# A four-layer decoder trunk on one core: norm vectors and the first stream block loaded through ScalarE's queue, weights first on SP's, the first weight block's high part copied by VectorE, ten warming products

## The chip, the core and the metric

The kernel runs on one core of a Trainium2 chip. The metric is the device time of one execution in microseconds (us); the times shown are medians of several executions. The core has five engines that run their own instruction lists in order and wait for each other through semaphores: TensorE (PE in the profile: PE is the matmul, PEld the load of its stationary operand), VectorE (DVE), ScalarE (ACT), GpSimd (POOL) and SyncE (SP). SP computes nothing here; it issues transfers between the chip's main memory and the on-chip memory. ScalarE can issue transfers too, from its own instruction list.

## The reference

A residual stream of 256 positions by 1024 features passes through four layers. Each layer normalises the stream, runs a token mixer, adds the result, normalises again, runs a squared-ReLU MLP of width 4096 and adds again. The mixers are, in turn, differential attention (layers 0 and 3), block-sparse attention (layer 1) and sliding-window attention (layer 2). Everything is float32.

```python
def rms_norm(x, g):
    xf = x.astype(jnp.float32)
    y = xf * lax.rsqrt(jnp.mean(xf * xf, axis=-1, keepdims=True) + NORM_EPS)
    return (y * g.astype(jnp.float32)).astype(x.dtype)

def sqrelu_mlp(h, w_up, w_down):
    a = jnp.maximum(h @ w_up, 0)
    return (a * a) @ w_down

def reference(x, positions, ...):
    cos, sin = rope_tables(positions)
    h = x
    for i in range(DEPTH):
        a = rms_norm(h, attn_norm_g[i])
        ...
        h = h + y
        h = h + sqrelu_mlp(rms_norm(h, mlp_norm_g[i]), mlp_w_up[i], mlp_w_down[i])
    return rms_norm(h, final_norm_g)
```

## The kernel before

The stream is kept transposed: features on the 128 partitions, positions along the free axis, as eight blocks of 128 features by 256 positions, two to a tile (`hT`, 128 by 512). The weights lie in main memory as pieces of 128 by 2048 in the order in which they are used, and are streamed through four buffers named `raw`.

Every product is made in three parts to keep float32's accuracy. `stage` (L153) splits a piece of weights into a high part `whi`, which ScalarE copies from `raw` in a reduced float32 format (L162), and a low part `wlo`, the difference, which VectorE computes (L163). `norm_part` (L309) does the same for a block of the stream: ScalarE multiplies it by its gain into the high part of `hg` (L315), VectorE computes the low part (L316). TensorE then adds high by high, low by high and high by low in one accumulator. The scale of the norm is applied after the product: `norm_sum` (L318) squares the stream on ScalarE (`sq`, L320) and adds on VectorE (`acc`, L325 and L329); `mean_square` makes `p_sum` and `nx` (L338), and GpSimd the factor `nr` (L291).

What matters here is the start of the program. SP issues, in this order: the norm vectors with the positions (`gn`, L197); then eight times a quarter of a weight piece (128 by 512, L148) followed by one block of the stream (128 by 256, L191), which makes pieces 0 and 1 and all eight blocks; then pieces 2 and 3 in halves (128 by 1024), and whole pieces from there on. Transfers take one of eight semaphores in turn, so from the ninth on an issue waits for the landing of the one eight before it. In the meantime VectorE begins the rotary tables (L239 to L254), which need `gn`, and GpSimd fills masks, constants and the zero halves of the key tiles (`kpadh`, `kpadl`, L456). TensorE multiplies a tile of ones by itself into `p_warm`, WARM = 12 times, and then starts the first projection `p_in` (L107, `proj` L362). The first projection runs feature block by feature block, six products for each (both halves of the positions with each of the three parts); call these groups 0 to 7. Group k needs quarter k of pieces 0 and 1 and block k of the stream. The second projection needs pieces 2 and 3, two feature blocks for each half-piece; I call the halves 2a, 2b, 3a and 3b.

The order on each engine is set by a scheduler when the program is built. `TURNS` (L36) adds, layer by layer, pairs of TensorE instructions of which the first must stand behind the second; instructions are counted by the accumulator that they write.

Of the kernel before, what the change touches and what calls it, by code (L numbers as in the profile page):

```python
# [27 lines left out]
NEG = -1.0e38  # L28
LOOK = 2
FAR = 5  # L30
WARM = 12
RAW = 4


# [14 lines left out]
        (("p_qk", 24), ("p_d", 5)),  # L49
        (("p_s", 40), ("p_d", 36)),  # L50
        (("p_t", 21), ("p_d", 66)),
    ),
    1: (
        (("p_sum", 0), ("p_in", 31)),
# [36 lines left out]

def f(ap):
    return ap.bitcast(F32)


class Numbered:
# [25 lines left out]
def trunk(ctx: ExitStack, tc: tile.TileContext, xT, gains, lams, swa_row, fng, weights, out):  # L122
# [18 lines left out]
    def fetch(parts=1, along=None):  # L141

        i = len(fetched)
        raw = sb.tile([P, 2048], F32, tag="raw", name=f"raw{i}", bufs=RAW)
        w = 2048 // parts
        for h in range(parts):
            s = slice(h * w, (h + 1) * w)
            nc.sync.dma_start(raw[:, s], weights[i, :, s])  # L148
            if along:
                along()  # L150
        fetched.append(raw)

    def stage(w=1024, first=None):  # L153
        i = len(staged)
        raw = fetched[i]
        hi = sb.tile([P, 2048], F32R, tag="whi", name=f"whi{i}", bufs=LOOK + 1)
        lo = sb.tile([P, 2048], F32R, tag="wlo", name=f"wlo{i}", bufs=LOOK + 1)
        for h in range(2048 // w):
            if first:
                first()  # L160
            s = slice(h * w, (h + 1) * w)
            A.activation(hi[:, s], raw[:, s], AF.Copy)  # L162
            V.tensor_tensor(lo[:, s], raw[:, s], f(hi[:, s]), op=OP.subtract)  # L163
        staged.append((hi, lo))

    used = [0]

    def take():
        i = used[0]
# [16 lines left out]
    posi = gn[:, 2 * DEPTH * 8 + 2:].bitcast(I32)  # L186
    loaded = []

    def load_x():
        d = len(loaded)  # L190
        nc.sync.dma_start(hT[d // 2][:, S * (d % 2):S * (d % 2) + S], xv[:, d, :])  # L191
        loaded.append(d)

    first_act = cst.tile([P, 1], F32, name="first_act")
    V.memset(first_act, 0.0)
    A.activation(first_act, first_act, AF.Copy)
    nc.sync.dma_start(gn, gains)  # L197
    fetch(4, load_x)
    fetch(4, load_x)
    fetch(2)  # L200
    fetch(2)

# [33 lines left out]
    def rotary_tables():  # L236
# [8 lines left out]
        for turn, bits in ((2.0 ** 16 * math.pi, 10), (2.0 * math.pi, 9), (2.0 * math.pi, 20)):  # L245
            q = cst.tile([P, NT, 8], F32, name="turns")
            V.tensor_scalar(q, an, 1.0 / turn, None, op0=OP.mult)
            V.tensor_scalar(q, q, 12582912.0, None, op0=OP.add)
            V.tensor_scalar(q, q, -12582912.0, None, op0=OP.add)
            for x in (an, an, lo):  # L250
                m, e = math.frexp(turn)
                c = math.ldexp(math.floor(m * 2 ** bits), e - bits)
                turn -= c
                V.scalar_tensor_tensor(x, q, -c, x, op0=OP.mult, op1=OP.add)  # L254
            if bits == 10:
                yield
            V.scalar_tensor_tensor(lo, q, -turn, lo, op0=OP.mult, op1=OP.add)
            if bits != 20:
                V.tensor_tensor(q, an, lo, op=OP.add)
                V.tensor_tensor(an, an, q, op=OP.subtract)  # L260
                V.tensor_tensor(lo, an, lo, op=OP.add)
                V.tensor_copy(an, q)
# [46 lines left out]
    def norm_part(n, d):  # L309

        j, b = d // 2, d % 2
        if b == 0:
            n.both.append(sb.tile([P, 2, 2, S], F32R, tag=f"hg{j}", name=f"hg{j}", bufs=1))
        both, h, g = n.both[j][:, b], hT[j][:, S * b:S * b + S], n.gain[:, d:d + 1]
        A.activation(both[:, 0], h, AF.Copy, scale=g)  # L315
        V.scalar_tensor_tensor(both[:, 1], h, g, f(both[:, 0]), op0=OP.mult, op1=OP.subtract)  # L316

    def norm_sum(n, j):  # L318
        sq = sb.tile([P, 512], F32, tag="relu", name="sq")
# [679 lines left out]
```

## Time and profile before

| what | value |
|---|---|
| median of 3 executions | 1141.2 us (1141.0 to 1141.56) |
| the profiled execution | 1141.6 us, span 1139.8 us |
| TensorE busy | 1130.4 us (99%) |
| VectorE busy | 826.2 us (72%) |
| ScalarE busy | 660.3 us (58%) |
| transfers | 198.66 MB, mean 174 GB/s |

The profile is one execution; times in it are counted from the start of its span. Each row of a timeline gives a start, a duration, the engine, the line of the kernel and the tiles as output<-inputs, and in brackets how long the engine had been idle and what released it. The profile's matmuls are pipelined and their ends are modelled, so a row of 0.39 us does not mean that the next product starts 0.39 us later; where it matters, the distance from start to start is used.

### The profile page before, as it was taken

Reading aid. Unit: us, or ns where it says so; the run is one execution under the profiler, and the core shown is the slowest. Engines: PE = TensorE matmul, PEld = TensorE weight load, DVE = VectorE, ACT = ScalarE, POOL = GpSimd, SP = SyncE. Lnnn points to the kernel's source line nnn. Section 1 sums busy time; section 2 is a strip of 40 time slices with the busy share of each in tenths; the row PEclk is TensorE's granted clock in tenths of the full one; section 3 lists DMA queues with packets and bytes.
Section 4 is the critical chain, followed back from the end, with each engine's and each line's share of the span. In section 5 each row is a group of like instructions: output and inputs, shape, how many; then the busy total and the mean of one; then the engine's idle time right before and its main releaser. Section 6 shows DMA issues by size and latency. Waiting matters only on the chain.

```text
span 1139.8 us, 17024 instructions
## 1 busy us (share of the span) xinstructions
PE 1130.4 (99%) x6560; PEld 982.9 (86%) x6560; DVE 826.2 (72%) x1584; ACT 660.3 (58%) x1207; POOL 13.2 (1%) x43
## 2 busy tenths in 40 slices
PE   9999999999999999999999999999999999999997
PEld 7889888888888888888899998888888889888886
DVE  7888977656676698766569887775667788777453
ACT  7866656544476665554446865554446776665342
POOL 2000000000000000000000000000000000000000
PEclk9999999999999999999999999999999999999999
DMA  8543455555544355555563346555554444554551
GB/s 321 206 148 116 171 198 193 196 198 185 185 148 148 112 185 188 188 200 191 194 209 111 112 149 222 185 185 187 189 197 139 144 142 162 197 195 168 185 185 37
DMA packets 30608, 198.66 MB, mean 174 GB/s; under 512 B 3520, under 2 KB 5184, under 8 KB 7360
## 3 DMA queue, kind: packets, MB, share of 16 engines
q1 hardware_dynamic: 30240, 197.06, 50.2%
q8 instruction: 51, 0.84, 0.3%
q10 hardware_dynamic: 288, 0.52, 0.1%
q14 instruction: 29, 0.24, 0.1%
HBM read 196.52 MB, written 1.05 MB: 173 GB/s over the span
## 4 chain that ended last, share of the span: by engine, by line
PE 94%; DVE 2%; DMA 1%; ACT 1%; issue 1%; SPq 0%; POOL 0%; POOLq 0%; DVEq 0%
PE p_up L107 31%; PE p_down L107 23%; PE p_in L107 18%; PE p_last L107 7%; PE p_d L107 6%; PE p_s L107 3%; PE p_av L107 2%; PE p_t L110 1%; DMA raw<-in_weights 1%; DVE wlo L163 1%; PE p_e L107 1%; PE p_qk L110 1%; ACT whi L162 0%; DVE kpadl L569 0%; ACT qk L680 0%
## 5 line engine op out<-in xcount | busy, mean ns | idle before, releaser
L163 DVE TENSOR_TENSOR wlo<-raw,whi 128x1024 fp32r<-128x1024 f32 (+1 forms) x374 | 446.5, 1210 | 201.8 <-ACT whi L162 200.9
L162 ACT ACTIVATE whi<-raw 128x1024 fp32r<-128x1024 f32 (+1 forms) x374 | 383.8, 1046 | 209.8 <-issue 110.5
L107 PE MATMUL p_up<-hg,whi 128*128 128x512 f32 x1024 | 356.1, 394 | 0.0
L107 PE MATMUL p_up<-hg,wlo 128*128 128x256 f32 x1024 | 283.1, 277 | 0.0
L107 PE MATMUL p_down<-uu,whi 128*128 128x512 f32 x768 | 266.4, 394 | 0.0
L107 PEld LDWEIGHTS p_up<-hg,whi 128*128 128x128 f32 x1024 | 191.8, 188 | 43.9
L107 PE MATMUL p_in<-whi,hg 128*128 128x512 f32 (+1 forms) x736 | 213.0, 371 | 0.4 <-ACT hg L315 0.4
L107 PE MATMUL p_down<-uu,wlo 128*128 128x256 f32 x768 | 212.7, 277 | 0.0
L107 PEld LDWEIGHTS p_up<-hg,wlo 128*128 128x128 f32 x1024 | 192.3, 188 | 0.5
L107 PEld LDWEIGHTS p_down<-uu,whi 128*128 128x128 f32 x768 | 144.0, 188 | 33.5
L107 PEld LDWEIGHTS p_in<-whi,hg 128*128 128x128 f32 x736 | 131.6, 189 | 24.0 <-ACT hg L315 1.1
L107 PEld LDWEIGHTS p_down<-uu,wlo 128*128 128x128 f32 x768 | 144.1, 188 | 0.0
L107 PE MATMUL p_in<-wlo,hg 128*128 128x512 f32 (+1 forms) x368 | 130.5, 368 | 0.6 <-DVE wlo L163 0.5
L107 PE MATMUL p_d<-oo,whi 128*128 128x256 f32 (+1 forms) x416 | 85.2, 296 | 0.0
L785 ACT ACTIVATE uu<-u 128x512 fp32r<-128x512 f32 x64 | 40.5, 632 | 73.5 <-DVE u L783 73.5
L107 PEld LDWEIGHTS p_in<-wlo,hg 128*128 128x128 f32 x368 | 68.8, 189 | 12.4 <-DVE wlo L163 1.5
L107 PE MATMUL p_last<-whi,uu 128*128 128x512 f32 (+1 forms) x264 | 79.4, 383 | 0.0
L705 ACT ACTIVATE cross<-p_up 128x256 f32<-128x256 f32 x128 | 47.9, 374 | 37.3 <-PE p_up L107 35.3
L107 PEld LDWEIGHTS p_d<-oo,whi 128*128 128x128 f32 x416 | 66.5, 191 | 2.5 <-issue 0.3
L315 ACT ACTIVATE hg<-hT,gn 128x256 fp32r<-128x256 f32 x64 | 31.4, 503 | 61.2 <-DVE hT L718 61.2
L426 ACT ACTIVATE e<-ns,nm 128x128 f32<-128x128 f32 (+1 forms) x128 | 56.7, 446 | 13.8 <-DVE nm L423 13.8
L107 PE MATMUL p_d<-oo,wlo 128*128 128x256 f32 x224 | 63.6, 287 | 0.0
(168 smaller groups left out, 1072.1 us busy)
## 6 DMA issues: line engine op xcount, KB each, us to landing
raw<-in_weights SPq DMA_DIRECT2D x181, 1024.0 KB, 4.9
raw<-in_weights SPq DMA_DIRECT2D x8, 256.0 KB, 4.6
raw<-in_weights SPq DMA_DIRECT2D x4, 512.0 KB, 7.8
hT<-in_xT SPq DMA_DIRECT2D x8, 128.0 KB, 4.5
bias<-in_swa_row SPq DMA_DIRECT2D x1, 512.0 KB, 3.7
grow<-in_fng SPq DMA_DIRECT2D x1, 512.0 KB, 3.5
out<-res SPq DMA_DIRECT2D x4, 128.0 KB, 2.1
out<-res ACTq DMA_DIRECT2D x2, 256.0 KB, 2.2
```

What stands on the lines that cost most here:

```text
L107: return self.keep(out.tensor.name.rstrip("_0123456789"), self.engine.matmul(out, *args, **kw))
L110: return self.keep(out.tensor.name.rstrip("_0123456789"), self.engine.transpose(out, *args, **kw))
L162: A.activation(hi[:, s], raw[:, s], AF.Copy)
L163: V.tensor_tensor(lo[:, s], raw[:, s], f(hi[:, s]), op=OP.subtract)
L315: A.activation(both[:, 0], h, AF.Copy, scale=g)
L426: A.activation(e[:, s], ns[:, s], AF.Exp, bias=nm[:, t:t + 1], scale=-1.0, accum_out=l[:, t:t + 1])
L705: A.activation(cross, p[:, S:], AF.Copy)
L785: A.activation(both[:, :, 0], r3(2)(u), AF.Copy)
```

## The change

Five things are changed, all of them at the program's start:

- `gn` and block 0 of the stream are issued by ScalarE, ahead of its first activation; SP's list begins with the first two quarters of weights, and a block of the stream follows each later quarter. SP has two transfers less to issue, and the order of the others is kept.
- The high part of the first quarter of weights is copied by VectorE (`tensor_copy`) and no longer by ScalarE.
- Three order rules on VectorE (`behind`): this copy stands behind the second of the angle operations of L254; the low part of the stream's block 0 behind the copy; the low part of the first weights behind that.
- WARM is 10 and no longer 12.
- `TURNS` has 22 more pairs for layer 0. The order of TensorE's list that results is that of before except in three short stretches. In the second projection, four products of half-piece 2b come before four of 2a, and the first product that reads the low part of 3a stands one place earlier. In the first scores, the first product that reads `kpadl` stands one place earlier. Near the end of the third projection two score products stand two places earlier. Beyond some 220 instructions of TensorE's list the lists of all engines are those of before.

```diff
--- before.py
+++ after.py
@@ -28,7 +28,7 @@
 NEG = -1.0e38
 LOOK = 2
 FAR = 5
-WARM = 12
+WARM = 10
 RAW = 4
 
 
@@ -49,6 +49,28 @@
         (("p_qk", 24), ("p_d", 5)),
         (("p_s", 40), ("p_d", 36)),
         (("p_t", 21), ("p_d", 66)),
+        (("p_sum", 0), ("p_in", 46)),
+        (("p_in", 47), ("p_sum", 1)),
+        (("p_in", 98), ("p_qk", 7)),
+        (("p_in", 114), ("p_s", 6)),
+        (("p_s", 4), ("p_in", 114)),
+        (("p_in", 115), ("p_s", 11)),
+        (("p_in", 116), ("p_s", 2)),
+        (("p_t", 0), ("p_in", 136)),
+        (("p_qk", 8), ("p_t", 0)),
+        (("p_t", 1), ("p_qk", 9)),
+        (("p_qk", 10), ("p_t", 2)),
+        (("p_in", 137), ("p_qk", 15)),
+        (("p_s", 12), ("p_in", 160)),
+        (("p_t", 3), ("p_s", 15)),
+        (("p_in", 161), ("p_t", 5)),
+        (("p_s", 13), ("p_in", 164)),
+        (("p_in", 165), ("p_s", 23)),
+        (("p_t", 6), ("p_in", 175)),
+        (("p_in", 176), ("p_t", 6)),
+        (("p_in", 178), ("p_t", 8)),
+        (("p_t", 9), ("p_in", 191)),
+        (("p_av", 0), ("p_t", 11)),
     ),
     1: (
         (("p_sum", 0), ("p_in", 31)),
@@ -93,6 +115,12 @@
     return ap.bitcast(F32)
 
 
+def behind(tc, late, ahead):
+
+    tc.add_manual_dep(late, ahead.name, mybir.DependencyInfo(mybir.DependencyClass.NoSync, mybir.DependencyReason.DATA),
+                      reason="behind")
+
+
 class Numbered:
 
 
@@ -147,7 +175,7 @@
             s = slice(h * w, (h + 1) * w)
             nc.sync.dma_start(raw[:, s], weights[i, :, s])
             if along:
-                along()
+                along(h)
         fetched.append(raw)
 
     def stage(w=1024, first=None):
@@ -156,14 +184,20 @@
         hi = sb.tile([P, 2048], F32R, tag="whi", name=f"whi{i}", bufs=LOOK + 1)
         lo = sb.tile([P, 2048], F32R, tag="wlo", name=f"wlo{i}", bufs=LOOK + 1)
         for h in range(2048 // w):
-            if first:
-                first()
+            normed = first() if first else None
             s = slice(h * w, (h + 1) * w)
-            A.activation(hi[:, s], raw[:, s], AF.Copy)
-            V.tensor_tensor(lo[:, s], raw[:, s], f(hi[:, s]), op=OP.subtract)
+            if i + h:
+                A.activation(hi[:, s], raw[:, s], AF.Copy)
+                V.tensor_tensor(lo[:, s], raw[:, s], f(hi[:, s]), op=OP.subtract)
+            else:
+
+                copied = V.tensor_copy(hi[:, s], raw[:, s]).ins
+                behind(tc, copied, angles[1])
+                behind(tc, normed, copied)
+                behind(tc, V.tensor_tensor(lo[:, s], raw[:, s], f(hi[:, s]), op=OP.subtract).ins, normed)
         staged.append((hi, lo))
 
-    used = [0]
+    used, angles = [0], []
 
     def take():
         i = used[0]
@@ -186,17 +220,18 @@
     posi = gn[:, 2 * DEPTH * 8 + 2:].bitcast(I32)
     loaded = []
 
-    def load_x():
+    def load_x(queue=nc.sync):
         d = len(loaded)
-        nc.sync.dma_start(hT[d // 2][:, S * (d % 2):S * (d % 2) + S], xv[:, d, :])
+        queue.dma_start(hT[d // 2][:, S * (d % 2):S * (d % 2) + S], xv[:, d, :])
         loaded.append(d)
 
     first_act = cst.tile([P, 1], F32, name="first_act")
     V.memset(first_act, 0.0)
+    nc.scalar.dma_start(gn, gains)
+    load_x(nc.scalar)
     A.activation(first_act, first_act, AF.Copy)
-    nc.sync.dma_start(gn, gains)
-    fetch(4, load_x)
-    fetch(4, load_x)
+    fetch(4, lambda h: h and load_x())
+    fetch(4, lambda h: load_x())
     fetch(2)
     fetch(2)
 
@@ -251,7 +286,7 @@
                 m, e = math.frexp(turn)
                 c = math.ldexp(math.floor(m * 2 ** bits), e - bits)
                 turn -= c
-                V.scalar_tensor_tensor(x, q, -c, x, op0=OP.mult, op1=OP.add)
+                angles.append(V.scalar_tensor_tensor(x, q, -c, x, op0=OP.mult, op1=OP.add).ins)
             if bits == 10:
                 yield
             V.scalar_tensor_tensor(lo, q, -turn, lo, op0=OP.mult, op1=OP.add)
@@ -313,7 +348,7 @@
             n.both.append(sb.tile([P, 2, 2, S], F32R, tag=f"hg{j}", name=f"hg{j}", bufs=1))
         both, h, g = n.both[j][:, b], hT[j][:, S * b:S * b + S], n.gain[:, d:d + 1]
         A.activation(both[:, 0], h, AF.Copy, scale=g)
-        V.scalar_tensor_tensor(both[:, 1], h, g, f(both[:, 0]), op0=OP.mult, op1=OP.subtract)
+        return V.scalar_tensor_tensor(both[:, 1], h, g, f(both[:, 0]), op0=OP.mult, op1=OP.subtract).ins
 
     def norm_sum(n, j):
         sq = sb.tile([P, 512], F32, tag="relu", name="sq")
```

## The prediction

> **What bounds the kernel now.** I read the page first, then TensorE's waits, then the chain of waits, then the timelines of the first 37 us, since the change touches nothing later.
>
> ```profile
> span 1139.8 us, 17024 instructions
> PE 1130.4 (99%) x6560; PEld 982.9 (86%) x6560; DVE 826.2 (72%) x1584; ACT 660.3 (58%) x1207; POOL 13.2 (1%) x43
> ```
>
> TensorE is busy for 99% of the span. Its waits over the whole span, apart from the one ahead of the warming products:
>
> ```profile
> PE p_s L107 <- DVE kpadl L569: 0.6, 3, 0.2
> PE p_in L107 <- DVE wlo L163: 0.5, 1, 0.5
> PE p_in L107 <- ACT hg L315: 0.4, 1, 0.4
> ```
>
> These are 1.5 us in all, so no change of the start can win much beyond an earlier first product and these waits. TensorE's timeline shows where they lie:
>
> ```profile
> 0.98 4.33 PE L107 MATMUL p_warm<-ones 128*128 128x128 f32 x24 [0.98 <-POOL ones L206]
> 5.70 1.46 PE L107 MATMUL p_in<-whi,hg 128*128 128x512 f32 x4 [0.39 <-ACT hg L315]
> 18.00 0.66 PE L107 MATMUL p_in<-whi,hg 128*128 128x512 f32 x2
> 19.18 0.50 PE L107 MATMUL p_in<-wlo,hg 128*128 128x512 f32 x1 [0.53 <-DVE wlo L163]
> 22.93 0.39 PE L107 MATMUL p_in<-wlo,hg 128*128 128x512 f32 x1
> 23.16 0.39 PE L107 MATMUL p_in<-whi,hg 128*128 128x512 f32 x1
> 23.62 0.50 PE L107 MATMUL p_in<-wlo,hg 128*128 128x512 f32 x1
> 35.77 0.40 PE L107 MATMUL p_in<-whi,hg 128*128 128x512 f32 x1
> 36.37 0.47 PE L107 MATMUL p_s<-kpadl,qhl 128*128 128x512 f32 x1 [0.20 <-DVE kpadl L569]
> ```
>
> One product follows the next by 0.23 us (22.93 to 23.16). The first projection starts at 5.70. At 18.00 come two products with the high part of half-piece 2a, and the low part lets the next start only at 19.18: 1.18 us for two products, 0.72 lost. Then 0.46 instead of 0.23 passes before 23.62 (low part of 3a), and 0.60 instead of 0.23 before 36.37. The chain of waits says what those three hang on:
>
> ```profile
> 10.17 6.62 DMA raw<-in_weights
> ...
> 16.81 1.07 ACT whi L162
> ...
> 17.90 1.22 DVE wlo L163
> 19.12 0.07 DVE nx L338
> ...
> 19.35 0.72 POOL nr L291
> ...
> 20.09 1.27 ACT qk L680 x2
> 21.36 0.96 ACT whi L162
> ...
> 23.48 1.22 DVE wlo L163
> ```
>
> It is one chain from the landing of 2a (16.79): its split on ScalarE and VectorE, the norm's factor, the scaling of `qk` that stands in ScalarE's list ahead of the split of 3a, that split. No TensorE work is in it. So from 19.18 to 36.37 TensorE runs at the pace of 2a's landing, and afterwards it waits for almost nothing. What the change is worth is how much earlier 2a lands, corrected for what the new order asks; not how much earlier the first product starts.
>
> **The change part by part.**
>
> Issues. SP's list and ScalarE's waits for weights:
>
> ```profile
> 0.73 0.38 SPq L197 DMA_DIRECT2D gn<-in_gains  x1
> 1.17 0.42 SPq L148 DMA_DIRECT2D raw<-in_weights  x1
> 2.10 0.44 SPq L148 DMA_DIRECT2D raw<-in_weights  x1
> 4.62 0.63 ACT L162 ACTIVATE whi<-raw 128x512 fp32r<-128x512 f32 x1 [2.40 <-DMA raw<-in_weights]
> 5.16 0.49 ACT L315 ACTIVATE hg<-hT,gn 128x256 fp32r<-128x256 f32 x1
> 16.81 1.06 ACT L162 ACTIVATE whi<-raw 128x1024 fp32r<-128x1024 f32 x1 [1.68 <-DMA raw<-in_weights]
> ```
>
> The first quarter is issued at 1.17 and will be issued at 0.73: 0.44 earlier. The second goes from 2.10 to about 1.17: 0.93 earlier, and all later ones of SP keep that lead until they wait for semaphores. On ScalarE `gn` goes out at its first free moment, about 0.73 as now, and block 0 one issue later, near 1.2 where SP issued it after the first quarter, near 1.6. ScalarE pays two issues of about 0.4 us (SP's rows) at a time when it waits 2.40 us for weights anyway; its table load and first activation, which stand behind them, slide by 0.9 into that wait. If that cover were gone it would cost 0.9.
>
> Does an earlier issue make 2a land earlier? The transfers' share, before they fill up:
>
> ```profile
> 2.00:3.00 1.00, 1.00 (x6) 1.00 (x6) 0.54 (x3) 0.21 (x2) 0.94 (x6) 1.00 0.55 153
> 3.00:4.00 1.00, 1.00 (x7) 1.00 (x6) 0.79 (x5) 0.00 (x0) 0.93 (x3) 1.00 0.77 263
> 8.00:10.00 2.00, 2.00 (x9) 1.35 (x8) 1.65 (x4) 2.00 (x5) 0.00 (x0) 1.00 1.00 319
> ```
>
> The last two numbers of a row are the share of the 16 transfer engines and GB/s. From 8 to 10 they are full, so from there the stream runs at its own pace, and 2a lands when all bytes ahead of it are through; those bytes do not change. From 2 to 4 the engines are 0.45 + 0.23 = 0.68 us idle, and that idle time is what an earlier issue can fill. The lead of 2a, L, is bounded below by 0.2 (the first quarter's 0.44, less what `gn` and block 0 now take from it in parallel; I see no way to a loss, since no byte is added) and above by 0.93 (two issues). I take 0.6: the 0.44 by which the first packets start, and a third of the remaining 0.49.
>
> The Trainium skill, "DMA: Bandwidth & Descriptors", section "Issuing engines are not separate DMA queues", says that transfers issued by several engines run on the same 16 engines and that only sequencer time is saved. By that alone the lead would be at most the 0.93 us, and 0.44 if the engines were the limit from the first packet.
>
> The copy. VectorE and GpSimd before the first group:
>
> ```profile
> 2.42 0.54 DVE L239 CAST posf<-gn 128x2 f32<-128x2 int32 x1 [1.56 <-DMA gn<-in_gains]
> 2.50 0.46 DVE L286 TENSOR_SCALAR gn<-gn 128x1 f32<-128x1 f32 x2
> 4.00 0.42 DVE L254 SCALAR_TENSOR_TENSOR an<-turns,an 128x16 f32<-128x16 f32 x2
> 5.28 0.69 DVE L163 TENSOR_TENSOR wlo<-raw,whi 128x512 fp32r<-128x512 f32 x1 [0.86 <-ACT whi L162]
> 5.89 0.48 DVE L316 SCALAR_TENSOR_TENSOR hg<-hT,gn,hg 128x256 fp32r<-128x256 f32 x1
> 2.47 0.42 POOL L221 MEMSET band<- 128x384 f32 x1
> 4.34 0.52 POOL L456 MEMSET kpadh<- 64x512 f32 x1
> 4.91 1.09 POOL L456 MEMSET kpadl<- 64x512 f32 x2
> ```
>
> The first quarter should land near 4.2 (4.62 less 0.44), but the copy stands behind the angle operations that end at 4.42. Its time is not in the trace: at most 0.69, the two-input operation of that size, at least 0.21, half of the row of 4.00, an operation on 16 columns. I take 0.5, nearer to the row of its own size. There is a catch in these rows. The CAST on two columns takes 0.54 us and both TENSOR_SCALAR end with it at 2.96, just after GpSimd's fill of 2.47 to 2.89, while the two-input operation of 5.28 keeps its 0.69 beside the fill of 4.91 to 6.00. So a one-input copy that starts at 4.42 can be held by the fill of 4.34 to 4.86. The high part is then there near 5.3, against 5.25 from ScalarE now; without the hold, near 4.9.
>
> The skill's page "Advanced Engine Details and Errata", section "VectorE Performance Modes", states this: VectorE's second port is shared with GpSimd, and two-port instructions block each other. It speaks against moving this copy. The same table lets a float32 copy take two elements in a cycle, by which an estimate is 0.3 us of streaming; the sum would then read 5.15 with the hold and 4.8 without.
>
> First product. `hg` of block 0 no longer stands behind the copy on ScalarE: block 0 lands some 0.45 earlier and its high part ends near 5.0 instead of 5.65. The first product starts when both are there, near 5.3 instead of 5.70. Ten warming products are 20 of the 24 rows; at even pace the last four take 0.7 of the 4.33 us, so they end near 4.6 instead of 5.31, ahead of the need. Behind the copy VectorE's queue holds block 0's low part (0.48), the first weights' low part (0.69), then block 1's. VectorE idles 0.86 us ahead of the 5.28 row today, which pays for the copy's 0.5.
>
> None of this counts at the end. Group 7 ends near 18.0 today, when the high part of 2a is also just ready (16.81 + 1.07 = 17.88). With the first product 0.4 earlier TensorE arrives near 17.6 and 2a's high part is ready at 17.88 - L = 17.3. The low part, 19.12 - L, still decides.
>
> New order. Both the first product on 3a's low part and the first on `kpadl` stand one place earlier. If their operands come at the old time less L, TensorE waits there as before and then has one product more to do: 0.23 lost, once, since the second limit lies on the same chain and the later one holds. The four products of 2b that come earlier have their operands (low part of 2b: a 1.22 operation behind 2a's) at a time when TensorE has not got there. I count their cost as nothing, covered by 2a's remaining products; uncovered it would be one more 0.23. WARM, the three rules on VectorE and the remaining pairs: nothing.
>
> **Sum.** 0.6 - 0.23 = 0.37 us earlier, say 0.4. Against the profiled execution's own 1141.6 us (span 1139.8 and 1.8 around it) that makes 1141.2; that execution is 0.4 above the median of the runs shown, 1141.2, so for the median I say **1140.8 us**. The 0.2% that a measurement of this kernel can tell from no change are 2.3 us; the sum lies far inside.
>
> **The rivals.**
>
> Rival 1: full lead and no order cost. SP's 0.93 arrives at 2a whole, because the early engines' 0.68 us of idle time is filled, and VectorE gets the low part of 3a early enough for its earlier place. For it: those idle shares. Against: the same chain sets 3a. Gain 0.9 to 1.2 (the 0.23 wait before 23.62 goes too): 1140.0 to 1140.3.
>
> Rival 2, on the other side: the stream does not move. The second queue's block 0 and `gn` take turns with the first quarter on the engines, which are already at 0.77 by 3 to 4 us, so 2a lands as before; then only the new order is left, 0.23 at 3a or at `kpadl`, plus up to 0.23 for the 2b stretch. Time 1141.2 + 0.2 to 0.5 = 1141.4 to 1141.7. It decides if L is below 0.23. For it: 319 GB/s full from 8 us on. Against: the first packets do start 0.44 earlier.
>
> Rival 3, slower as well: the copy waits for all fills of GpSimd, to 6.00, and ends near 6.5. The first product then starts 0.8 later than now. TensorE arrives near 18.8, against the low part of 2a at 18.5 to 19.1: cost 0 to 0.3, 1140.8 to 1141.5. It decides only beyond 0.7 of lateness, and what comes free in VectorE's list after 6 us makes up for part of it.
>
> Rival 4: everything that is idle now closes, 0.4 at the start, 0.72, 0.23 and 0.37 at the three waits: 1.7 us, 1139.5. Against: 2a would have to land 1.7 earlier, twice what SP can give.
>
> **How the numbers follow.** Forecast (0.2 to 0.6 gained, 1140.6 to 1141.0) 0.55; rival 1 0.2; rival 2 0.15; rival 3 0.05, mostly near no change; rival 4 0.03; 0.02 for what I have not seen. The range takes in rivals 1 and 2: **1139.9 to 1141.6 us**. Every case but the last stays within 2.3 us of 1141.2, so within 0.2% gets 0.92; faster 0.05, half of rival 4 and what might go beyond it; slower 0.03.
>
> **What would show it.** SP's first issue at about 0.73 should be weights; ScalarE's wait before the split of 2a should end 0.2 to 0.9 ahead of 16.81. The copy's row should start near 4.4 and end near 5.3 if GpSimd's fills hold it, near 4.9 if not. The first `p_in` should stand near 5.3. The low part of 2a should be the wait that ends last, near 18.6. If 2a lands early and the end does not move, the order has eaten it, and the waits before 3a and `kpadl` must be longer. Wrong altogether if the wait after 18 us is gone, or if the clock or the transfers differ after 40 us.

## The result, and the profile after

| | median | executions |
|---|---|---|
| before | 1141.05 us | 20, from 1140.88 to 1141.84 |
| after | 1142.91 us | 20, from 1141.65 to 1144.2 |
| ratio after to before | 1.0013 | 95% interval 1.0007 to 1.0019 |

The change makes the kernel slower by 1.86 us in the median; the forecast was 0.4 us faster. That is less than the 0.2% taken as no change, but the interval leaves 1 out. The executions of after do not scatter evenly: six lie at 1141.65 to 1141.93 and thirteen at 1142.67 to 1143.03, with one at 1144.2. I call these the lower and the upper level. They differ by 1.2 us. Before has no such gap: sixteen of its executions lie at 1140.88 to 1141.25 and four at 1141.53 to 1141.84. A few executions of either kernel, such as one of 4085 us in run 5, take far longer and are no part of the argument.

The profile of after that came with the result is one execution on the lower level, 1141.69 us. Its span and shares:

```profile
span 1139.9 us, 17014 instructions
PE 1129.7 (99%) x6556; PEld 983.2 (86%) x6556; DVE 826.5 (73%) x1585; ACT 659.7 (58%) x1206; POOL 13.2 (1%) x43
```

The span is 0.1 us longer than the one of before shown above (an execution of 1141.56 us, one of the four longer ones). TensorE's timeline in this profile (start, duration, engine, line, operation, tiles; in brackets the idle time ahead and its releaser):

```profile
0.98 4.64 PE L135 MATMUL p_warm<-ones 128*128 128x128 f32 x20 [0.98 <-POOL ones L241]
7.13 1.16 PE L135 MATMUL p_in<-whi,hg 128*128 128x512 f32 x4 [1.51 <-ACT hg L350]
...
17.67 0.39 PE L135 MATMUL p_in<-wlo,hg 128*128 128x512 f32 x1
17.90 0.60 PE L135 MATMUL p_sum<-ones,acc 128*128 128x128 f32 x4
...
18.58 0.63 PE L135 MATMUL p_in<-whi,hg 128*128 128x512 f32 x2
19.04 0.47 PE L135 MATMUL p_in<-wlo,hg 128*128 128x512 f32 x1
...
22.20 0.49 PE L135 MATMUL p_in<-whi,hg 128*128 128x512 f32 x1 [0.25 <-ACT whi L190]
```

The first product starts at 7.13 instead of 5.70 and not at the forecast 5.3. Its row names ScalarE's `hg`, but that ended at 6.10; what came last was VectorE's copy, and the row of run 6 (below) names it in the same place. The low part of 2a is no longer waited for (before: 0.53 us ahead of 19.18). VectorE's and ScalarE's timelines show what came late:

```profile
4.60 0.27 DVE L274 CAST posf<-gn 128x2 f32<-128x2 int32 x1 [3.75 <-DMA gn<-in_gains]
...
5.48 0.54 DVE L283 TENSOR_SCALAR turns<-turns 128x16 f32<-128x16 f32 x1
6.05 0.17 DVE L284 TENSOR_SCALAR turns<-turns 128x16 f32<-128x16 f32 x1
6.26 0.38 DVE L289 SCALAR_TENSOR_TENSOR an<-turns,an 128x16 f32<-128x16 f32 x2
6.56 0.42 DVE L194 CAST whi<-raw 128x512 fp32r<-128x512 f32 x1
...
17.75 1.22 DVE L191 TENSOR_TENSOR wlo<-raw,whi 128x1024 fp32r<-128x1024 f32 x1
```

```profile
0.73 0.41 ACTq L230 DMA_DIRECT2D gn<-in_gains  x1
1.17 0.45 ACTq L225 DMA_DIRECT2D hT<-in_xT  x1
...
5.59 0.51 ACT L350 ACTIVATE hg<-hT,gn 128x256 fp32r<-128x256 f32 x1 [2.44 <-DMA hT<-in_xT]
...
15.25 1.07 ACT L190 ACTIVATE whi<-raw 128x1024 fp32r<-128x1024 f32 x1 [0.48 <-DMA raw<-in_weights]
...
19.93 1.27 ACT L715 ACTIVATE qk<-p_in,nr 128x512 f32<-128x512 f32 x2 [2.35 <-POOL nr L326]
21.09 2.96 ACT L190 ACTIVATE whi<-raw 128x1024 fp32r<-128x1024 f32 x3
```

`gn` is issued at 0.73, the moment at which SP issued it, but VectorE gets it at 4.60 and not at 2.42. The packets in the two traces show the way there: in before the 128 rows of 272 bytes that make up `gn` pass alone, from 1.73 to 2.06; in after they pass from 1.93 to 4.07, between rows of 2 KB of the weights, which begin at 1.74. Block 0 gets to ScalarE at 5.59 instead of 5.16. The angle operations end at 6.64, and the copy, which has to stand behind them, runs only then. The weights are early: the split of 2a starts at 15.25 instead of 16.81. The transfers' share in the first full stretch shows the weights coming in:

```profile
2.00:3.00 1.00, 1.00 (x6) 1.00 (x6) 0.00 (x0) 0.99 (x2) 0.95 (x5) 1.00 0.93 217
3.00:4.00 1.00, 1.00 (x7) 1.00 (x6) 0.00 (x0) 0.15 (x1) 0.93 (x3) 1.00 0.86 273
```

0.93 and 0.86 instead of 0.55 and 0.77: the engines carry more weights than before, and in after the rows of `gn` stand among them.

### The profile page after: what moved, and what is told of

The parts are those of the page before. It is cut to its first block, busy times and chain, and to the rows that moved or that the text cites. A ratio compares the mean times of both kernels' runs of the same rounds, so it can differ in the third digit from the quotient of the medians.

```text
span 1139.9 us, 17014 instructions
## 1 busy us (share of the span) xinstructions
PE 1129.7 (99%) x6556; PEld 983.2 (86%) x6556; DVE 826.5 (73%) x1585; ACT 659.7 (58%) x1206; POOL 13.2 (1%) x43
## 4 chain that ended last, share of the span: by engine, by line
PE 94%; DVE 2%; ACT 2%; issue 1%; DMA 0%; POOL 0%; POOLq 0%; ACTq 0%; DVEq 0%
PE p_up L135 31%; PE p_down L135 23%; PE p_in L135 18%; PE p_last L135 7%; PE p_d L135 6%; PE p_s L135 3%; PE p_av L135 2%; PE p_t L138 1%; DVE wlo L191 1%; PE p_e L135 1%; PE p_qk L138 1%; ACT whi L190 1%; DMA hT<-in_xT 0%; DVE kpadl L604 0%; ACT hg L350 0%
## 5 line engine op out<-in xcount | busy, mean ns | idle before, releaser
L740 ACT ACTIVATE cross<-p_up 128x256 f32<-128x256 f32 x128 | 48.0, 375 | 37.4 <-PE p_up L135 35.4
```

Of the source, the lines that this page charges most:

```text
L740: A.activation(cross, p[:, S:], AF.Copy)
```

## The experiments

Two questions: what makes the first product late and what that costs, and where the upper level comes from. Theory V says that `gn`, issued beside the weights, lands late, and that all else follows. Theory C says that TensorE's idle stretch between warming products and first product lets its clock fall in some executions. In each group of runs the kernel before was timed on the same chip. Unless something else is said, each run was timed 10 or 11 times.

### 1. `gn` back to SP (e1)

```diff
-    nc.scalar.dma_start(gn, gains)
+    nc.sync.dma_start(gn, gains)
```

> The changed kernel with the norm vectors issued by SP again, first in its list; block 0 of the stream stays on ScalarE's queue, WARM is 10. Theory V (the small vectors' transfer, alone ahead of the weights before, now takes turns with 2 KB rows of weights on the same transfer engines and lands at 4.6 instead of 2.4 us, and the angle operations, the copy behind them and the first product slide with it): the first VectorE operation on the vectors starts near 2.4, the copy ends by 5.3, the first product of the projection starts near 5.3 to 5.7, and the time falls from 1142.9 to between 1140.4 and 1141.3. Theory C (ten warming products alone are too few to raise TensorE's clock): the first product moves likewise, but the times still lie on two levels 1.2 us apart, median above 1141.6. Theory O (the new pairs of TensorE's order cost the time): above 1142.

Measured: 1141.10 us against 1141.29 for before, ratio 0.9999 (0.9990 to 1.0008). The first product starts at 5.86. One of eleven lies at 1142.88 and one at 1142.62; the other nine at 1140.5 to 1141.4. The scheduler also ordered some products otherwise, as it did in runs 3, 8 and 11; run 7 removes this. VectorE's timeline in this run settles another point:

```profile
4.89 0.82 DVE L194 CAST whi<-raw 128x512 fp32r<-128x512 f32 x1 [0.47 <-DMA raw<-in_weights]
```

The copy that takes 0.42 us at 6.56, after GpSimd's fills, takes 0.82 here, beside them.

### 2. Ten warming products alone (e2)

The kernel before with `WARM = 10`.

> The kernel before with WARM = 10 and nothing else; all engines' orders are those of before. Theory C: at least 0.6 us slower than before (1141.65 or more), on two levels, with the rise of the clock later than 3.9 us in the profile. Theory V: the same as before within 0.2 us (1140.9 to 1141.3), since the gap ahead of the first product grows by 0.7 us only.

Measured: 1141.46 us, 1140.87 to 1142.01, ratio 1.0000 (0.9991 to 1.0009), no second level. With the first product at 5.60, warming that ends at 5.62 leaves no gap. Alone, this edit costs nothing that this timing can tell.

### 3. No rule behind the angles (e3)

```diff
-                behind(tc, copied, angles[1])
```

> The changed kernel without the rule that puts the copy behind the second angle operation. Theory V: the copy then starts as the first quarter of weights lands, near 4 us, but block 0 of the stream lands at 5.5 and its high part ends at 6.1, so the first product comes near 6.1 instead of 7.13; the low part of block 0 and that of the first weights stand ahead of the angle operations or behind them; time 1141.2 to 1142.0. If the copy on VectorE itself is the cost, no change: 1142.5 to 1143.

Measured: 1141.48 us (1141.39 to 1142.98), ratio 1.0002 (0.9994 to 1.0011); two of eleven executions are above 1142. The copy ran at 5.05, ahead of the angle operations, and the first product still came at 6.97: it then waited for block 0, whose high part started at 6.41 (5.59 in after). So the rule holds the copy, but the landings on ScalarE's queue held the first product almost as long in this execution, one of 1142.98 us.

### 4. Sixteen warming products (e4)

The changed kernel with `WARM = 16`.

> The changed kernel with WARM = 16. Theory C in its wider form (the gap between the last warming product and the first product of the projection, 1.5 us and more, lets the clock rise late in most executions): the upper level near 1142.9 goes, the median falls to 1141.7 or below; the first product does not move by more than 0.2 us. Theory V alone: the median stays at 1142.5 to 1143. The scheduler moves a few products of the second projection and the first scores, worth 0.3 us at most.

Measured: 1142.89 us, all eleven within 1142.80 to 1142.99, ratio 1.0013 (1.0004 to 1.0022). This is no test of theory C: the scheduler took the extra products as a reason to order VectorE, ScalarE and TensorE otherwise, and TensorE then waited 0.76 us at 25.1 for a low part. From here on, the runs called "same order" have the order of the changed kernel's first 321, 140 and 90 instructions on TensorE, VectorE and ScalarE written out as pairs, so that nothing but the named edit moves.

### 5. The changed kernel, same order (e5)

> The changed kernel itself, its order written out, so the same program: a second sample and another profile. Both theories: two levels again, near 1141.7 and near 1142.9 us, more than half of the executions on the upper one, median 1141.7 to 1143. Theory C (the idle stretch ahead of the first product lets the TensorE clock fall): a profile on the upper level shows products p_in of the first two groups at about 0.45 us a piece instead of 0.23 and the first p_sum 1.2 to 1.7 us later than 17.9; a profile on the lower level shows full pace from the first product on. Rival (the levels come from transfers or from VectorE's list): a profile on the upper level has full pace in those groups and a longer wait behind them.

Measured: nine executions, three at 1141.63 to 1141.66 and six at 1142.70 to 1142.99: the two levels again. This run has no profile of one of the nine.

### 6. Sixteen warming products, same order (e6)

> The changed kernel with 16 warming products instead of 10 and nothing else moved on any engine, so that the idle 1.5 us ahead of the first product is filled. Theory C: the upper level is gone, all executions at 1141.5 to 1142.0 us, first product at 7.1 to 7.2 us. Rival (levels from elsewhere): two levels stay, 1141.7 and 1142.9 us. Rival that the warming products delay the first product: one level, later by what the first product is later than 7.13.

Measured: 1141.67 us, all ten within 1141.63 to 1141.76; ratio 1.0000 (0.9991 to 1.0009). TensorE's timeline:

```profile
0.98 5.21 PE L140 MATMUL p_warm<-ones 128*128 128x128 f32 x32 [0.98 <-POOL ones L264]
7.11 1.17 PE L140 MATMUL p_in<-whi,hg 128*128 128x512 f32 x4 [0.92 <-DVE whi L140]
...
17.88 0.60 PE L140 MATMUL p_sum<-ones,acc 128*128 128x128 f32 x4
```

First product and `p_sum` stand where after has them, and the upper level is gone. Six products that no result needs take 1.1 to 1.2 us off the median of the changed kernel (1142.91 in its own timing, 1142.74 for the nine of run 5).

### 7. `gn` on SP, same order (e7)

The edit of run 1 with the order kept.

> The changed kernel with the norm vectors' load issued first on SP's queue instead of ScalarE's and nothing else moved on any engine. Theory V (the late landing of the norm vectors makes the first product late): they land near 2.7 us, the first product comes at 5.8 to 5.9, the first p_sum near 17.5, and the time is 1140.7 to 1141.4 us, with at most few executions above 1142. Rival (their landing does not matter, the stream order sets the time): 1141.7 and 1142.9 as the changed kernel.

Measured: 1141.09 us (1140.86 to 1141.66) against 1141.67 (1141.63 to 1141.76) for run 6, timed with it, and 1141.25 for before; ratio to before 0.9999 (0.9990 to 1.0009). Run 6 has sixteen warming products and this one ten; against the three lower executions of run 5, which differ in the edit alone, the step is the same to 0.02 us. ScalarE's, VectorE's and TensorE's timelines:

```profile
0.73 0.41 ACTq L248 DMA_DIRECT2D hT<-in_xT  x1
...
3.06 0.51 ACT L140 ACTIVATE hg<-hT,gn 128x256 fp32r<-128x256 f32 x1 [0.39 <-DMA hT<-in_xT]
```

```profile
2.87 0.17 DVE L140 CAST posf<-gn 128x2 f32<-128x2 int32 x1 [2.01 <-DMA gn<-in_gains]
...
5.23 0.50 DVE L140 CAST whi<-raw 128x512 fp32r<-128x512 f32 x1 [0.80 <-DMA raw<-in_weights]
```

```profile
5.88 1.17 PE L140 MATMUL p_in<-whi,hg 128*128 128x512 f32 x4 [0.26 <-DVE whi L140]
...
17.62 0.60 PE L140 MATMUL p_sum<-ones,acc 128*128 128x128 f32 x4
...
22.08 0.50 PE L140 MATMUL p_in<-whi,hg 128*128 128x512 f32 x1 [0.26 <-ACT whi L140]
```

One transfer of 34 KB, moved back ahead of the weights, brings the first product from 7.13 to 5.88 and the median down by 0.58 us, and none of the ten executions is on the upper level. Theory V holds for the first product. The queue of ScalarE is not slow in itself: block 0, 128 KB, issued there at 0.73 ahead of the weights, is used at 3.06.

What the 0.58 us consist of is another matter. The product on 3a's high part starts at 22.08 against 22.20 in after, and the span, 1139.8, is 0.2 shorter than that of run 6: these profiles are of executions of 1141.55 and 1141.76. The executions of run 7 lie in two groups, seven at 1140.86 to 1141.22 and three at 1141.55 to 1141.66; all ten of run 6 lie beside the longer group. So the start accounts for 0.1 to 0.2 us as far as the profiles show, and the rest is that most executions of run 7 are in the shorter group. Run 13 has a profile of a short execution.

### 8. Copy back on ScalarE (e8)

```diff
-            if i + h:
-                A.activation(hi[:, s], raw[:, s], AF.Copy)
-                V.tensor_tensor(lo[:, s], raw[:, s], f(hi[:, s]), op=OP.subtract)
-            else:
...
+            A.activation(hi[:, s], raw[:, s], AF.Copy)
+            V.tensor_tensor(lo[:, s], raw[:, s], f(hi[:, s]), op=OP.subtract)
```

> The changed kernel with the first weights' high part copied by ScalarE as before, without the order behind the angles; queues, written-out order and ten warming products as changed. If VectorE's copy and its place behind the angles hold the first product: it comes at 6.2 to 6.6 us and the time is 1141.0 to 1141.6. If the landings on ScalarE's queue hold it: the first product still waits for the stream block and the norm vectors, at 6.7 to 7.5 us, and the time stays at 1141.4 to 1142.9 with two levels.

Measured: 1141.40 us (1141.35 to 1142.92, two of ten above 1142), ratio 1.0004 (0.9995 to 1.0013). TensorE's timeline:

```profile
6.03 0.73 PE L135 MATMUL p_in<-whi,hg 128*128 128x512 f32 x2 [0.41 <-ACT hg L344]
7.58 0.73 PE L135 MATMUL p_in<-whi,hg 128*128 128x512 f32 x2 [0.82 <-DVE hg L345]
```

Neither side was quite right. Two products start at 6.03, when block 0 has landed; the next wait until 7.58 for block 0's low part, which stands behind late angle operations and the first weights' low part in VectorE's list. In this profile the copy's engine decides when the first two products start, the late `gn` when the rest does.

### 9 and 10. The changed kernel twice more (e9, e10)

> The changed kernel once more, for a profile of an execution on its upper level (1142.6 to 1143.1 us). Theory C: there the TensorE clock rises near 4 us, falls back in the idle stretch ahead of the first product, and the products p_in of the first groups take about 0.45 us a piece instead of 0.23, with p_sum 1.2 to 1.7 us later than 17.9. Rival: full pace from the first product on, and a longer wait behind 18 us. If the execution falls on the lower level (1141.6 to 1141.9) it says nothing new.

> As the run before it, a second look for the upper level: theory C expects half-pace products in the first groups wherever the time is 1142.6 to 1143.1 us, and full pace from the first product on wherever it is 1141.6 to 1141.9; the rival expects full pace in both.

Measured: 1142.86 and 1141.64 us, one of each level. TensorE's timeline of the one at 1142.86:

```profile
0.98 3.85 PE L135 MATMUL p_warm<-ones 128*128 128x128 f32 x20 [0.98 <-POOL ones L241]
7.11 1.92 PE L135 MATMUL p_in<-whi,hg 128*128 128x512 f32 x4 [2.28 <-ACT hg L350]
8.83 1.05 PE L135 MATMUL p_in<-wlo,hg 128*128 128x512 f32 x2
9.68 1.54 PE L135 MATMUL p_in<-whi,hg 128*128 128x512 f32 x4
...
19.49 0.60 PE L135 MATMUL p_sum<-ones,acc 128*128 128x128 f32 x4
...
23.46 0.50 PE L135 MATMUL p_in<-whi,hg 128*128 128x512 f32 x1 [0.15 <-ACT whi L190]
```

and of the one at 1141.64:

```profile
0.98 4.63 PE L135 MATMUL p_warm<-ones 128*128 128x128 f32 x20 [0.98 <-POOL ones L241]
7.12 1.17 PE L135 MATMUL p_in<-whi,hg 128*128 128x512 f32 x4 [1.50 <-DVE whi L194]
...
17.89 0.60 PE L135 MATMUL p_sum<-ones,acc 128*128 128x128 f32 x4
...
22.18 0.50 PE L135 MATMUL p_in<-whi,hg 128*128 128x512 f32 x1 [0.24 <-ACT whi L190]
```

The first product starts at the same time in both. In the slower one the warming products, the same twenty rows, end 0.78 us sooner, because the clock rose while they ran (they follow each other by 0.21 us at first and by 0.11 from 3.89 on), and the idle stretch is 2.28 us. Then six products take from 7.11 to 9.68, 0.43 a piece instead of 0.25 (7.12 to 8.59), and `p_sum` is 1.60 us later. Of this, 1.28 are left at 3a (23.46 against 22.18) and 1.2 at the end. The windows of the slower one show the clock (the third number from the right):

```profile
7.00:8.00 1.00, 0.89 (x3) 0.72 (x4) 1.00 (x3) 1.00 (x4) 0.00 (x0) 0.63 1.10 318
8.00:9.00 1.00, 1.00 (x4) 0.81 (x3) 1.00 (x3) 1.00 (x4) 0.00 (x0) 0.50 0.79 251
9.00:10.00 1.00, 1.00 (x4) 0.81 (x3) 1.00 (x3) 1.00 (x3) 0.00 (x0) 0.50 0.92 323
10.00:11.00 1.00, 1.00 (x4) 0.76 (x4) 1.00 (x3) 1.00 (x3) 0.00 (x0) 0.66 1.03 324
```

At half clock, 0.63 in a window means 0.74 us of it at half, 0.66 means 0.68; with the two full windows that is 3.42 us, from 7.26 to 10.68. The clock records in the traces agree and begin with the rise: full clock from 3.85 to 7.26 in this run, and in run 3, an execution of 1142.98 us, from 4.11 to 7.52, then half until 10.93. (The column shows 1.00 ahead of the rise too; there the pace of the rows tells.) Theory C holds for the two executions of the upper level that were profiled, and run 6, which fills the stretch, has no upper level. Not every time near 1142.9 is of this kind: the profiles of run 4 (1142.86) and run 12 (1142.90) have full clock from the first product to past 1100 us.

### 11. The queues alone (e11)

The kernel before with the changed queues only.

> The kernel before with only its queues changed (norm vectors and first stream block issued by ScalarE, weights first on SP's): copy on ScalarE, twelve warming products and the old written-out order stay. Theory V: the norm vectors land near 4.2 to 4.6 us and the block near 5.4 instead of 2.4 and 5.1, the second products come at 7 us or later, and the queues alone cost 0.1 to 0.7 us (1141.3 to 1142.0), with few executions at 1142.9. Rival (VectorE's copy and its place behind the angles are the whole loss): 1140.4 to 1140.9, faster than the kernel before.

Measured: 1141.45 us (1141.08 to 1141.55) against 1141.18, ratio 1.0003 (0.9994 to 1.0013). `posf` starts at 4.53, so `gn` lands as late as in after. The second pair of products starts at 7.56. The loss is some 0.3 us, as theory V has it, but the interval includes 1; there is no upper level with twelve warming products. The scheduler moved some products here too (`p_sum` stands ahead of the last group), so this is not quite the queues alone.

### 12. Both repaired (e12)

`gn` first on SP, two blocks of the stream on ScalarE's queue, the copy on ScalarE, twelve warming products, angle operations moved back on VectorE.

> Norm vectors first on SP's queue, the first two stream blocks on ScalarE's, the copy back on ScalarE, twelve warming products, and VectorE's order fixed so that the angle operations ahead of the third weights' first low part come behind it. If VectorE's list is what eats the lead of the stream, then TensorE runs from 5.6 to 5.9 us without the holes of 0.1 to 0.6 us that the kernel with the norm vectors on SP has up to 12 us, p_sum comes at 16.6 to 17.3 and the time is 1140.0 to 1140.7 us, better than both. Rival (TensorE has no more to win here, or the weights come too late for it): 1141.0 to 1141.5.

Measured: 1141.78 us (1141.28 to 1142.90), ratio 1.0007 (0.9997 to 1.0016). A miss: with one block less between them the weights did not come earlier. The split of 2a started at 16.86, as in before, and TensorE waited 0.57 us for it and 0.70 and 0.65 at 3a. Several things were changed at once, and I draw no more from this run than one row, used in run 14.

### 13. Twelve warming products, same order (e13)

> The changed kernel with the twelve warming products of before and nothing else moved on any engine. If the edit of WARM from 12 to 10 is what lets the clock fall, the upper level is gone, and all executions lie at 1141.5 to 1142.0 us. If the late first product alone is enough (an idle stretch of some 1.1 to 1.8 us is left even with twelve), the upper level stays, with executions at 1142.6 to 1143.1.

Measured: 1141.68 us, all ten within 1141.23 to 1141.77, ratio 1.0004 (0.9994 to 1.0013). With the share of upper executions that after shows (14 of 20), ten in a row on the lower level are no accident. So the upper level needs both edits: the late first product makes the gap, and the two warming products taken away make it long enough. In this run's profile the clock rose during the warming too, at 4.25, and 1.64 us of idle time did not bring it down.

The profile is of the one short execution, 1141.23 us. Its first product and its product on 3a start where run 6 has them (7.11 and 22.18), yet its span is 0.5 shorter. The difference arises between 388 and 426 us, on ScalarE's timeline of run 6 and of this run:

```profile
388.29 1.07 ACT L140 ACTIVATE whi<-raw 128x1024 fp32r<-128x1024 f32 x1
...
426.19 0.39 ACT L140 ACTIVATE cross<-p_up 128x256 f32<-128x256 f32 x1 [0.26 <-PE p_up L140]
```

```profile
388.29 1.07 ACT L140 ACTIVATE whi<-raw 128x1024 fp32r<-128x1024 f32 x1
...
425.70 0.39 ACT L140 ACTIVATE cross<-p_up 128x256 f32<-128x256 f32 x1 [0.18 <-PE p_up L140]
```

The profile of run 11, of its one short execution, needs 37.4 us between these two rows as this one does; the other fourteen profiles that can be used need 37.8 to 37.9. No edit reaches that stretch, and nothing here shows what decides it.

### 14. Angle operations out of the way (e14)

Run 7 with six angle operations moved behind both low parts of the third weights on VectorE.

> The changed kernel with the norm vectors first on SP's queue and six angle operations of VectorE (about 1.1 us of its list between 16.7 and 19.3 us) moved behind both low parts of the third weights; nothing else differs from the run with the norm vectors on SP. If VectorE's list is what keeps the stream's lead from TensorE: the low part of half-piece 2a starts at 17.0 to 17.2 instead of 17.63, the hole ahead of its product closes, and the time is 1140.6 to 1140.9 us. If TensorE's own list holds by then: 1141.0 to 1141.3 as that run.

Measured: 1141.76 us (1141.36 to 1142.57), ratio 1.0006 (0.9996 to 1.0015), in the median slower than run 7. In the profiled execution `gn` was first used at 3.38 and the first product came at 6.42, both later than in run 7. VectorE did what was wanted all the same: the low part of 2a started at 16.52. But TensorE then waited 1.02 us for the high part of 3a, whose product started at 22.01, where run 7 has it. GpSimd's and ScalarE's timelines show why:

```profile
18.16 1.55 POOL L349 TENSOR_TENSOR nr<-nx,minus_half 128x2 f32<-128x2 f32 x1 [12.16 <-DVE nx L140]
```

```profile
19.74 1.27 ACT L140 ACTIVATE qk<-p_in,nr 128x512 f32<-128x512 f32 x2 [2.59 <-POOL nr L349]
20.90 2.95 ACT L140 ACTIVATE whi<-raw 128x1024 fp32r<-128x1024 f32 x3
```

The factor `nr` takes 1.55 us here. It starts while VectorE's 1.23 us low part of 2b is running (17.92 to 19.15). In after, two small angle operations stood between `nx` and that low part, and `nr` got in ahead of it, at 19.19 against 19.24, and took 0.71. Run 12 shows the long one again: `nr` starts at 19.41, the low part of 2b at 19.25, and `nr` takes 1.63. In all other profiles that can be used it takes 0.71.

### 15. Two small operations put back between (e15)

Run 14 with two of its six moved operations put back between `nx` and the low part of 2b, and with twelve warming products.

> The run before with two of the six moved angle operations put back between nx and the low part of 2b, and twelve warming products. Theory G (GpSimd's nr is held by VectorE's 1.23 us operation when it starts beside it, as in the run before, where it took 1.55 us instead of 0.71): nr takes 0.7 us again and starts near 18.2, the split of 3a starts before 20.5 instead of 20.9, the wait ahead of the first product on 3a falls from 1.02 to under 0.4 us, and the time is 1140.5 to 1141.0, faster than the run with the norm vectors on SP. Rival (the split of 3a waits for the products of 2a or for weights, not for nr): the wait stays near 1 us and the time at 1141.2 to 1141.8.

Measured: 1141.06 us against 1141.06 for before, ratio 0.9999 (0.9990 to 1.0008). GpSimd's and TensorE's timelines:

```profile
18.57 0.71 POOL L349 TENSOR_TENSOR nr<-nx,minus_half 128x2 f32<-128x2 f32 x1 [12.37 <-DVE an_lo L140]
```

```profile
21.58 0.50 PE L140 MATMUL p_in<-whi,hg 128*128 128x512 f32 x1 [0.25 <-ACT whi L140]
```

`nr` is back at 0.71, the wait at 0.25, and the product on 3a starts at 21.58, 0.6 earlier than in after and 0.5 earlier than in run 7. The mechanism was as expected; the time, with two edits against run 14, falls short of the 1140.5 to 1141.0 expected. Its product on 3a is the earliest here, and its time is not faster than before by anything that could be measured.

## Why the prediction was wrong

**What bounds the kernel.** Right for before: the chain from 2a's landing. After the change it no longer did. Between 7.13 and 22 us TensorE runs nearly without a hole from its first product on, up to the split of 3a. That split hangs on the low part of 2a, `nx` and `nr`, which now wait for VectorE's list and no longer for the landing.

**Issues.** This is the step that failed. The prediction said that `gn` goes out on ScalarE "at its first free moment, about 0.73 as now" and went on with the issue as if it were the landing. The issue was at 0.73. The first use went from 2.42 to 4.60. In before, `gn` is alone for 0.44 us ahead of the first weights in the same queue; in after, the first weights are issued in the same moment by the other queue. The prediction named this sharing, but let it slow the weights by a little and not `gn` by 2.2 us. Block 0 went the same way: it was to land 0.45 earlier, and its high part starts at 5.59 instead of 5.16. Run 7 shows the cause by moving this one transfer: first use at 2.87, first product at 5.88.

The passage that the prediction takes from the Trainium skill, "DMA: Bandwidth & Descriptors", section "Issuing engines are not separate DMA queues", was the right warning, read for the wrong transfer. Transfers of several queues run on the same engines and interleave, so what was moved past the weights in issue order loses the lead that its place in the queue gave it. The traces agree: 4.60 (after) and 4.53 (run 11) on the second queue, 2.87 (run 7) at the head of the same one; over all profiles 4.2 to 4.6 and 2.8 to 3.4.

**The lead of 2a.** Mis-sized: 0.6 was taken, with 0.93 as the upper bound; the split of 2a moved by 1.56. In the windows from 2 to 4 us the engines are busy for 0.47 us more than before, where the prediction counted on no more than 0.68 of idle time to fill. 2a was issued at 9.13 instead of 10.17 and took 6.1 us instead of 6.6 from issue to landing: 1.04 of the 1.56 are the issue, little more than the two issues saved. Why the flight was 0.5 shorter is open. The lead bought little: the low part of 2a started at 17.75 instead of 17.90, because VectorE's list, begun 2.2 us later, reached it only then.

**The copy.** The hold by GpSimd's fills is real (0.82 us beside them in run 1, 0.42 after them), and the estimate of 0.5 was near. But in after the copy ran at 6.56, when the fills had ended; what held it was the rule behind the angles, costed at "nothing". The fills cost it time all the same: the angle operation of 5.48 takes 0.54 beside them, its like at 6.05, after them, 0.17. Run 3 shows that without the rule block 0 can hold the first product until 6.97 anyway. (A slip in the prediction's second sum: 4.42 and 0.3 make 4.7 without the hold, not 4.8.)

**The first product.** Forecast near 5.3, measured at 7.13. That this does not count at the end came out half right. The 1.43 us of lateness against before's profile shrink to 0.58 at `p_sum` (17.90 against 17.32 in before), since groups that start late run dense, and to 0.1 in the span, since the wait of 0.53 ahead of 2a's low part is gone. But the profile of before, 1141.56 us, was one of its longer executions: 0.4 above the median that the prediction used, 0.5 above that of all 20. Against this median the lower level, near 1141.7, is 0.65 us slower; beside runs 6 and 13, which lie on this level, before is 0.42 and 0.55 faster. The 0.1 of the spans is what the profiles show of this; the rest, some 0.5, is the shorter group of executions, in which most of before and of run 7 lie, and of after, run 6 and run 13 one in 26. Whether the late `gn` keeps them out of it, and how, is open.

**WARM.** Costed at nothing, because warming would end "ahead of the need". This is the second step that failed, and the dearer one. Its end was put at 4.6 by an even pace of the rows, which they do not have. It ended at 4.83 to 5.62; the need came at 7.1. The price is 1.2 us in two of three executions (runs 6, 9 and 13). The prediction gave the clock no chance at all ahead of 40 us. Of the 1.86 us of the median, 1.2 are thus the clock, which fell because of the late first product and the two products taken away together; of the 0.65 left, 0.1 are seen at the start, and the rest is not explained.

**New order.** Costed at 0.23. In after 0.65 us instead of 0.23 pass ahead of 22.20, where the high part of 3a is first read; before lost 0.23 ahead of 23.62, at the low part. That is 0.2 more, near the forecast, but no run changes the order alone, so whether the order makes it is not shown. What ends last there is the split of 3a, behind the scaling of `qk` in ScalarE's list (19.93 and 21.09 in after). Run 14 shows that an earlier VectorE alone moves nothing past this point, since `nr` took longer.

**The rivals.** Rival 3 had the right picture, a copy that is too late and a first product that is late by more than 0.7, with a chance of 0.05 and the wrong cause. It took that lateness for harmless up to 0.3 us, which the profiles bear out as long as the clock stays up. (The range was to take in rival 2, whose upper end, 1141.7, lies 0.1 outside.)

## What to carry to other kernels

A transfer's place in a queue is part of its latency: before a small, early-needed load goes to another queue, ask what will be issued beside it in the same moment, and price the landing from a row, not the issue. Warming products should last until the first real product: whenever the first product can move, look at the gap between both in several executions, since the moment at which the clock rises varies from one to the next (3.85 to 7.14 us in the profiles here). And where an order was tuned by hand, small operations between two large ones can be what lets another engine in; in run 14, with two of them moved away, `nr` took 0.84 us longer, and the earlier products of 2a gained nothing.

## What was not expected of the hardware

- TensorE's clock, once up, fell after 3.41 us although TensorE had been busy for a part of them. In run 9 the clock was up from 3.85 to 7.26, with warming until 4.83 and products from 7.11: 1.1 us busy. In run 3 it was up from 4.11 to 7.52, with warming until 4.95 and products from 6.97: 1.4 us busy. In run 13 it rose at 4.25 and stayed up; in the 3.41 us from there TensorE was busy for 1.8 us, until 5.47 and from 7.11. The idle stretches were 2.28, 2.01 and 1.64 us. That the busy share of such a window decides is an inference from these three, not a run of its own. After its fall the clock was at half for 3.41 us under full load. The Trainium skill, "TensorE: Matmul & The Clock Gate", Part 1, has a free-running window of about 3.4 us; the length agrees. Its advice in "Why this matters for your kernels", no idle gaps above about 3 us, does not hold here, as 2.0 us were enough.
- GpSimd's operation on 128 by 2 elements took 1.55 us instead of 0.71 when it started 0.24 us into a VectorE operation of 1.23 us (run 14), and 1.63 when it started 0.16 into one (run 12). VectorE's one-input operations are held by GpSimd's fills (0.82 for 0.42 us), which looks like the same contention from the other side.
- Far from every edit, the same work between 388 and 426 us took 37.4 us in two profiles and 37.8 to 37.9 in the fourteen others (run 13). Half a microsecond in the medians here need not come from the start.
